# Per-head keys in a latent-attention trunk: one 128-row VectorE multiplication, with key rows and rope key copied into one tile by DMA

## The chip, the core and the metric

The kernel runs on one core of one Trainium2 chip. The core has five engines, each with its own row of instructions that it takes in order: TensorE (PE: matmuls, and PEld for the weight loads that overlap them), VectorE (DVE), ScalarE (ACT), GpSimd (POOL) and SyncE (SP, which here only issues DMAs). Data lies in HBM, in SBUF (128 partitions, written "rows" below) and in PSUM, where matmuls write. The metric is the device time of one execution in microseconds (us); the median of several is compared. A profile is one further execution, recorded by the hardware profiler.

## What is computed

Two layers over 528 tokens (16 meta tokens and 512 others), 1024 channels. Each has a pooling branch and an attention branch with 8 heads; each head's key has 64 channels of its own and 32 rotary channels that all heads share. Both are normalized together, per head and token:

```python
k_nope, v = kv[..., :QK_NOPE_DIM], kv[..., QK_NOPE_DIM:]
k_pe = jnp.broadcast_to(k_rope_raw[:, :, None, :], (B, L, N_HEADS, QK_ROPE_DIM))
k = jnp.concatenate([k_nope, k_pe], axis=-1)
q = rmsnorm(q, g_qn)
k = rmsnorm(k, g_kn)
q = jnp.concatenate([q[..., :QK_NOPE_DIM], apply_rope(q[..., QK_NOPE_DIM:], pos)], axis=-1)
k = jnp.concatenate([k[..., :QK_NOPE_DIM], apply_rope(k[..., QK_NOPE_DIM:], pos)], axis=-1)
o = causal_block_attention(q, k, v)
```

All of it is float32. The attention's output is gated, projected, merged with the pooling branch and added to the residual stream.

## The kernel before

**Precision.** Every product is made of three matmuls (`mm3`, lines 188, 191 and 192): both factors are split into a high part (a ScalarE copy to fp32r, `whi`, `kh`, `th`) and a remainder (a VectorE subtraction, `wlo`, `kl`, `tl`), and high x high, high x low and low x high are summed in PSUM. So every weight tile that is loaded (`raw`, line 115, three buffers) costs ScalarE one copy (line 183) and VectorE one subtraction (line 184) before TensorE can use it, and its buffer is free for the next load after the subtraction.

**What sets the order.** The program is written as one stream of weight tiles (`stream`, `plan`), into which the attention's work is put at points given by counted matmul time (`step`, `fill`, `after`). The instruction order on each engine is then decided by a scheduler that plays the program through with its own estimates of durations; so a changed instruction can shift others around it. On the chip, each engine takes its row in order and waits on semaphores.

**Keys.** All tiles hold channels in rows and tokens in columns (528). A pair p of heads has a tile `kn[p]`: rows 0 to 63 hold the 64 own channels of the even head 2p, rows 64 to 127 those of the odd head 2p+1 (`ev_k`). `kp` holds the 32 rotary channels four times over, in rows 0 to 127 (`rope`, lines 534 and 535, GpSimd). The norm's factor per head and token is a row in HBM (`kdr`); `spread_k` (line 838) broadcasts it over 128 rows into `bc`, two heads ahead, on SyncE's queue.

**prep(h)** (line 842) makes one head's key: a tile `kf` whose 64 own rows are kn[p] x bc, a VectorE multiplication (line 849), and whose other 64 rows are kp x bc, a GpSimd multiplication (line 850). An even head has its own rows in 0 to 63 and the rotary ones in 64 to 127, an odd head the other way round; the matching rows of the query tile `qhl` are zero where a rotary copy is not wanted. `kf` is then split into `kh` (ScalarE, line 297) and `kl` (VectorE, line 298), and the query's rows are put together, the rotary ones by two DMAs between SBUF tiles (line 860).

**head(h)** (line 863) makes the scores S from `kh`, `kl` and `qhl`, masks them and finds the row minimum on VectorE (line 879), takes the exponential on ScalarE (line 886), and divides by the row sums on GpSimd (lines 924 and 926). `pv` transposes the probabilities on TensorE (line 946), splits them, and multiplies by the values (951, 952). Between these stand the weight stream's matmuls. prep(h+1) comes about half way through head h. In layer 1 the stream that runs beside the attention is made of sums and differences of gate weights (`fast`, lines 601 to 646), which give VectorE more to do per matmul.

Of the kernel before, what the change touches and what calls it, by code (L numbers as in the profile page):

```python
# [72 lines left out]
def trunk(ctx, tc, xT, pos, win, wkr, wqb, wkb, wvb, wgr, wpu, wmu, wout, gains, const, yT):  # L73
    nc = tc.nc
    pe, act, dve, gp, sp = nc.tensor, nc.scalar, nc.vector, nc.gpsimd, nc.sync
# [11 lines left out]
    def nm(s):  # L87
        uid[0] += 1
        return f"{s}_{uid[0]}"

    def slot(tag, dt=F32, bufs=1, w=W):
        return sl.tile([P, w], dt, tag=tag, name=nm(tag), bufs=bufs)

    def tmp(w=W):
        return tp.tile([P, w], F32, tag="tmp", name=nm("tmp"), bufs=3)
# [200 lines left out]
    def split(hi, lo, src, a, b):  # L296
        act.activation(hi[:, a:b], src, AF.Copy)  # L297
        dve.tensor_sub(lo[:, a:b], src, hi[:, a:b].bitcast(F32))  # L298
# [5 lines left out]
    def newton(y, a, t):  # L304
        dve.tensor_single_scalar(y.bitcast(I32), a.bitcast(I32), 1, op=ALU.logical_shift_right)
        dve.tensor_scalar(y.bitcast(I32), y.bitcast(I32), -1.0, float(0x5F3759DF), op0=ALU.mult, op1=ALU.add)
        dve.tensor_scalar(a, a, -0.5, None, op0=ALU.mult)
        for _ in range(3):
            dve.tensor_mul(t, y, y)
            dve.tensor_mul(t, t, a)  # L310
            dve.scalar_tensor_tensor(out=y, in0=t, scalar=1.5, in1=y, op0=ALU.add, op1=ALU.mult)
# [47 lines left out]
    class Layer:  # L359
# [158 lines left out]
        def k_factors(self):  # L518
            flat = lambda d: d.rearrange("h (s c) -> (h s) c", c=T // 16)
            na, ny, nt = (sm.tile([P, T // 16], F32, tag=t, name=nm(t)) for t in ("ka", "ky", "kt"))  # L520
            sp.dma_start(na, flat(ksr[self.l]))
            dve.tensor_scalar(na, na, 1.0 / QK, EPS, op0=ALU.mult, op1=ALU.add)
            newton(ny, na, nt)
            sp.dma_start(flat(kdr[self.l]), ny)
            self.bcs = {}
            for h in range(2):
                self.spread_k(h)

        def rope(self, out, src, a, b):
            n = b - a  # L530
            t = tmp()
            dve.stream_shuffle(t[:, :n], src, SWAP)
            dve.tensor_mul(t[:, :n], t[:, :n], tsin[:, a:b])
            gp.tensor_mul(src, src, tcos[:, a:b])
            gp.tensor_add(out, src, t[:, :n])
# [302 lines left out]
        def spread_k(self, h):  # L838
            self.bcs[h] = bc = slot("bc", bufs=3)
            sp.dma_start(bc, kdr[self.l][h:h + 1, :].partition_broadcast(P))  # L840

        def prep(self, h):
            p, odd = h // 2, h % 2
            n0, r0 = (64, 0) if odd else (0, 64)
            kf = tmp()
            bc = self.bcs.pop(h)
            if h + 2 < H:
                self.spread_k(h + 2)
            dve.tensor_mul(kf[n0:n0 + 64, :], self.kn[p][n0:n0 + 64, :], bc[n0:n0 + 64, :])
            gp.tensor_mul(kf[r0:r0 + 64, :], self.kp[r0:r0 + 64, :], bc[r0:r0 + 64, :])  # L850
            kh, kl = slot("kh", F32R, bufs=2), slot("kl", F32R, bufs=2)
            split(kh, kl, kf[:, :T], 0, T)
            qh, ql = qhl[odd]
            x0 = self.x0
            src = self.qn[p][n0:n0 + 64, x0:T]
            act.activation(qh[n0:n0 + 64, x0:T], src, AF.Copy)
            dve.tensor_sub(ql[n0:n0 + 64, x0:T], src, qh[n0:n0 + 64, x0:T].bitcast(F32))
            g0 = 32 * (h % 4)
            for d, f in zip((qh, ql), self.qr[h // 4]):
                sp.dma_start(d[r0:r0 + 32, x0:T].bitcast(F32), f[g0:g0 + 32, x0:T].bitcast(F32))  # L860
            return kh, kl, qh, ql
# [551 lines left out]
```

## Time and profile before

| | us |
|---|---|
| median of 3 runs (lowest, highest) | 786.03 (784.74, 787.63) |
| the profiled execution: its time | 788.06 |
| the profiled execution: span, first to last instruction | 786.2 |
| attention of layer 0 in it (first and last key multiplication) | 154 to 285 |
| attention of layer 1 in it | 531 to 677 |
| granted TensorE clock, mean | 1.000 |

In the profile's lines, `L184 DVE TENSOR_TENSOR wlo<-raw,whi 128x512` is the VectorE instruction of line 184 that writes a tile `wlo` from `raw` and `whi`. Groups give the count (x16), busy time, mean duration, and idle time of the engine before them with what ended it. A row of a timeline gives start and duration in us. A row of waits gives who waited for whom: us in total, times, longest. A matmul's end is modelled, so starts are safer to read than ends.

### The profile page before, as it was taken

The numbers are of one execution on the slowest core, as the hardware profiler recorded it, in microseconds if no ns is written. First come the engines' busy times: TensorE is split into PE (matmuls) and PEld (weight loads), VectorE is DVE, ScalarE is ACT, GpSimd is POOL, SyncE is SP. The second block draws the span as 40 slices with busy tenths as digits, with TensorE's granted clock in tenths as the row PEclk, the third lists the DMA queues.
The fourth block names the chain that finished last, engine by engine and source line by source line (L and its number), as shares of the span: only waits on it lengthen the run. The fifth ranks groups of instructions, "written<-read, shape, count | busy, mean of one in ns | idle before, by whom it ended". The sixth has DMA issues, their size and how long they took to land.

```text
span 786.2 us, 15369 instructions
## 1 busy us (share of the span) xinstructions
PE 774.8 (99%) x5469; PEld 711.1 (90%) x5469; DVE 587.0 (75%) x1316; ACT 446.7 (57%) x1022; POOL 230.2 (29%) x319
## 2 busy tenths in 40 slices
PE   9999999999999999999999999999999999999998
PEld 8999899999999999999997898887788899788887
DVE  5848788547778977689764477775997899974984
ACT  8545655645556665545664356455667676654462
POOL 1024514203434342211320245131026235240213
PEclk9999999999999999999999999999999999999999
DMA  6242367765645465565653423435456566562655
GB/s 243 82 97 87 103 163 165 180 154 136 144 120 138 120 135 150 135 187 155 172 151 92 102 81 95 125 88 181 121 132 162 160 168 164 150 212 88 213 148 136
DMA packets 64909, 110.76 MB, mean 141 GB/s; under 512 B 10544, under 2 KB 16560, under 8 KB 64832
## 3 DMA queue, kind: packets, MB, share of 16 engines
q1 hardware_dynamic: 54928, 90.02, 38.4%
q0 software_dynamic: 8896, 17.92, 12.6%
q10 hardware_dynamic: 1008, 1.84, 0.6%
q8 instruction: 43, 0.70, 0.4%
q14 instruction: 34, 0.28, 0.1%
HBM read 100.18 MB, written 22.62 MB: 156 GB/s over the span
## 4 chain that ended last, share of the span: by engine, by line
PE 84%; DVE 6%; DMA 4%; issue 2%; ACT 2%; POOL 0%; SPq 0%; DVEq 0%; ACTq 0%
PE mm L188 24%; PE mm L192 23%; PE mm L191 23%; DVE wlo L184 2%; PE S L188 2%; PE S L191 2%; PE S L192 2%; PE mm L946 2%; DMA raw<-wsumgp 1%; DMA raw<-win 1%; PE o L952 1%; PE o L951 1%; PE S L500 1%; ACT whi L183 1%; DMA raw<-wqb 1%
## 5 line engine op out<-in xcount | busy, mean ns | idle before, releaser
L188 PE MATMUL mm<-hh,whi 128*128 128x264 f32 (+2 forms) x992 | 306.0, 311 | 1.6 <-DVE tmp L637 0.6
L192 PE MATMUL mm<-hh,wlo 128*128 128x264 f32 (+2 forms) x992 | 304.1, 309 | 1.1 <-DVE wlo L184 1.0
L191 PE MATMUL mm<-hl,whi 128*128 128x264 f32 (+2 forms) x992 | 304.5, 308 | 0.0
L184 DVE TENSOR_TENSOR wlo<-raw,whi 128x512 fp32r<-128x512 f32 (+2 forms) x261 | 191.9, 739 | 98.1 <-ACT whi L183 94.3
L183 ACT ACTIVATE whi<-raw 128x512 fp32r<-128x512 f32 (+2 forms) x261 | 156.5, 603 | 165.9 <-PE mm L191 91.0
L188 PEld LDWEIGHTS mm<-hh,whi 128*128 128x128 f32 x992 | 186.2, 188 | 12.9 <-issue 1.2
L192 PEld LDWEIGHTS mm<-hh,wlo 128*128 128x128 f32 x992 | 185.8, 188 | 10.6 <-DVE wlo L184 2.3
L191 PEld LDWEIGHTS mm<-hl,whi 128*128 128x128 f32 x992 | 186.8, 188 | 9.1
L188 PE MATMUL mm<-cq,whi 128*128 128x264 f32 (+2 forms) x140 | 44.2, 316 | 1.3 <-ACT racc L960 0.7
L192 PE MATMUL mm<-cq,wlo 128*128 128x264 f32 (+2 forms) x140 | 43.5, 313 | 0.6 <-DVE wlo L184 0.6
L191 PE MATMUL mm<-cq,whi 128*128 128x264 f32 (+2 forms) x140 | 43.5, 312 | 0.0
L879 DVE CUSTOM_DVE_ANT_0 S<-S,maskw,nqs 128x288 f32<-128x288 f32 (+4 forms) x80 | 38.4, 497 | 2.5 <-PE S L192 2.2
L702 POOL TENSOR_TENSOR racc<-racc,tmp 128x264 f32<-128x264 f32 (+1 forms) x15 | 14.3, 951 | 87.2 <-ACT tmp L701 87.1
L188 PE MATMUL mm<-u,whi 128*128 128x264 f32 (+1 forms) x108 | 35.3, 327 | 0.1
L192 PE MATMUL mm<-u,wlo 128*128 128x264 f32 (+1 forms) x108 | 34.8, 322 | 0.0
L298 DVE TENSOR_TENSOR tl<-mm,th 128x512 fp32r<-128x512 f32 (+1 forms) x64 | 29.2, 481 | 7.4 <-ACT th L297 6.3
L850 POOL TENSOR_TENSOR tmp<-kp,bc 64x528 f32<-64x528 f32 x16 | 25.6, 1602 | 30.5 <-issue 15.4
L353 POOL DMA_DIRECT2D wsum<-wout x8 | 6.9, 859 | 89.0 <-PE mm L192 73.0
L924 POOL TENSOR_TENSOR pm<-pa,rs 128x16 f32<-128x16 f32 x32 | 11.0, 345 | 72.6 <-DVE rs L919 66.7
L926 POOL TENSOR_TENSOR cq<-cq,rs 128x384 f32<-128x384 f32 (+1 forms) x32 | 32.2, 1005 | 0.0
L886 ACT ACTIVATE cq<-S,bia 128x400 f32<-128x400 f32 (+2 forms) x48 | 24.6, 515 | 12.2 <-DVE bia L914 7.2
L297 ACT ACTIVATE th<-mm 128x512 fp32r<-128x512 f32 (+1 forms) x64 | 25.9, 432 | 8.4 <-PE mm L946 7.3
(333 smaller groups left out, 1722.0 us busy)
## 6 DMA issues: line engine op xcount, KB each, us to landing
raw<-win SPq DMA_DIRECT2D x139, 256.0 KB, 3.0
raw<-wout SPq DMA_DIRECT2D x22, 256.0 KB, 3.5
bc<-kdr SPq DMA_DIRECT2D x16, 264.0 KB, 4.2
wsum<-wout SPq DMA_DIRECT2D x16, 256.0 KB, 3.5
raw<-wpu SPq DMA_DIRECT2D x16, 256.0 KB, 3.1
wsumgp<-win SPq DMA_DIRECT2D x16, 256.0 KB, 3.3
raw<-wmu SPq DMA_DIRECT2D x16, 256.0 KB, 2.7
raw<-wsumgp SPq DMA_DIRECT2D x16, 256.0 KB, 3.8
```

The lines of the kernel that those rows point to most:

```text
L183: act.activation(hi[:, :n], raw[:, :n], AF.Copy)
L184: dve.tensor_sub(lo[:, :n], raw[:, :n], hi[:, :n].bitcast(F32))
L188: first = pe.matmul(out, wh, xh, start=start, stop=False, skip_group_check=more)
L191: pe.matmul(out, wh, xl, start=False, stop=False, skip_group_check=more)
L192: newest[0] = pe.matmul(out, wl, xh, start=False, stop=stop, skip_group_check=more)
L297: act.activation(hi[:, a:b], src, AF.Copy)
L298: dve.tensor_sub(lo[:, a:b], src, hi[:, a:b].bitcast(F32))
L850: gp.tensor_mul(kf[r0:r0 + 64, :], self.kp[r0:r0 + 64, :], bc[r0:r0 + 64, :])
L879: dve.tensor_tensor_reduce(out=sv, in0=sv, in1=mask, scale=nqs[:, i, h:h + 1], scalar=3e38, op0=ALU.add, op1=ALU.min, accum_out=bia[:, c:c ...
L886: act.activation(pv, sv, AF.Exp, scale=-1.0, bias=bia[:, i:i + 1], accum_out=rs[:, c:c + 1])
L926: gp.tensor_mul(pt[i][:, NM:], pt[i][:, NM:], rs[:, i:i + 1].to_broadcast([P, n - NM]))
L946: pe.transpose(tr[:, P * (i - j):P * (i - j + 1)], pt[i][:, NM + P * j:NM + P * (j + 1)], ident)
```

## The change

```diff
@@ k_factors, after the loop over spread_k(0), spread_k(1)
+            self.lend(0)
 
@@ beside spread_k
+        def lend(self, p):
+            sp.dma_start(self.kp[0:64, :], self.kn[p][0:64, :])
+
         def prep(self, h):
             p, odd = h // 2, h % 2
             n0, r0 = (64, 0) if odd else (0, 64)
@@ in prep
             bc = self.bcs.pop(h)
             if h + 2 < H:
                 self.spread_k(h + 2)
-            dve.tensor_mul(kf[n0:n0 + 64, :], self.kn[p][n0:n0 + 64, :], bc[n0:n0 + 64, :])
-            gp.tensor_mul(kf[r0:r0 + 64, :], self.kp[r0:r0 + 64, :], bc[r0:r0 + 64, :])
+            dve.tensor_mul(kf, self.kn[p] if odd else self.kp, bc)
+            if not odd:
+                sp.dma_start(self.kn[p][0:64, :], self.kp[64:128, :])
+            elif p < 3:
+                self.lend(p + 1)
```

A pair's first copy (`lend`) puts the even head's own rows into rows 0 to 63 of `kp`, whose rows 64 to 127 keep the rotary key: `kp` is then the whole key of the even head. The second copy puts the rotary key from `kp` into rows 0 to 63 of `kn[p]`, whose rows 64 to 127 hold the odd head's own channels. Each head is then one VectorE multiplication over all 128 rows. Per layer there are 8 copies of 64 x 528 float32. The first copy of pair p+1 waits for the multiplication of head 2p, which reads `kp`; the second copy of a pair waits for the first one, which reads the rows it overwrites.

The scheduler's order changes with it. On SyncE, in layer 1's attention, the rows around the broadcast (`bc`) for head 6 stood like this before (`raw` are weight tiles, `kdr` the norm factors; numbers tell buffers apart and may differ by one between the two programs):

```order
L115 DMA raw_8565<-wsumgp_124 128x512
L840 DMA bc_8764<-kdr_122 128x528
L115 DMA raw_8585<-wsumgp_124 128x512
L115 DMA raw_8639<-win 128x512
L115 DMA raw_8661<-win 128x512
```

In the changed program (its line numbers are higher by 1 to 7) the same place reads:

```order
L115 DMA raw_8566<-wsumgp_124 128x512
L841 DMA bc_8765<-kdr_122 128x528
L844 DMA kp_6474<-kn_1215_6722 64x528
L115 DMA raw_8586<-wsumgp_124 128x512
L855 DMA kn_1215_6722<-kp_6474 64x528
L115 DMA raw_8640<-win 128x512
L115 DMA raw_8662<-win 128x512
```

Both copies of the last pair stand among the weight loads, right behind the broadcast that is set free by head 4's multiplication, with one weight load between them; two weight loads stand behind the second copy. In the other pairs the second copy follows the first directly (the first two pairs of each layer), or with one to three DMAs between.

On TensorE, the first score products of head 6 of layer 1 (S from `kh_9005` before, `kh_9006` in the changed program) stood at the end of a gate tile's 24 matmuls (`mm_9104`, `mm_9105`), which before began and ended so:

```order
L188 MATMUL mm_9104<-hh_6_132,whi_9058 128x512
L191 MATMUL mm_9104<-hl_7_133,whi_9058 128x512
L192 MATMUL mm_9104<-hh_6_132,wlo_9059 128x512
...
L192 MATMUL mm_9104<-hh_20_146,wlo_9101 128x512
L952 MATMUL o_8865<-tl_9025,vt 128x128
L946 MATMUL mm_9122<-cst,pa_8814 128x128
L188 MATMUL S_9082<-kh_9005,qhl_105 128x272
L188 MATMUL S_9091<-kh_9005,qhl_105 128x400
```

In the changed program the tile begins:

```order
L188 MATMUL mm_9105<-hh_6_132,whi_9059 128x512
L191 MATMUL mm_9105<-hl_7_133,whi_9059 128x512
L188 MATMUL S_9083<-kh_9006,qhl_105 128x272
L188 MATMUL S_9092<-kh_9006,qhl_105 128x400
L188 MATMUL S_9173<-kh_9006,qhl_105 128x288
L192 MATMUL mm_9105<-hh_6_132,wlo_9060 128x512
L188 MATMUL mm_9105<-hh_8_134,whi_9059 128x512
```

The three products with `kh` moved ahead of 22 of the tile's matmuls; those with `kl` follow at the tile's end, as before. Similar moves stand at heads 3 and 5 of layer 1 and, smaller ones, at heads 2 and 3 of layer 0. The rows of GpSimd keep their order without the sixteen multiplications.

## The prediction

> **What bounds the kernel now.** First the page: busy times, then the chain that ended last.
>
> ```profile
> span 786.2 us, 15369 instructions
> ...
> PE 774.8 (99%) x5469; PEld 711.1 (90%) x5469; DVE 587.0 (75%) x1316; ACT 446.7 (57%) x1022; POOL 230.2 (29%) x319
> ...
> PE 84%; DVE 6%; DMA 4%; issue 2%; ACT 2%; POOL 0%; SPq 0%; DVEq 0%; ACTq 0%
> ```
>
> TensorE is busy for 99% of the span and carries 84% of the chain. The change takes no matmul away, so it can only win where TensorE stands still. The busy times by stretch say where that is.
>
> ```profile
> core 0: us, PE busy (x) PEld busy (x) DVE busy (x) ACT busy (x) POOL busy (x), PEclk, DMA share, GB/s
> 200.00:220.00 20.00, 20.00 (x165) 19.78 (x165) 15.80 (x42) 12.23 (x31) 7.68 (x11) 1.00 0.61 145
> 640.00:660.00 20.00, 19.79 (x141) 18.30 (x140) 19.82 (x44) 14.79 (x38) 8.56 (x11) 1.00 0.57 131
> ```
>
> In layer 0's attention (200 to 220 us stands for it) TensorE has no idle time: eight of the sixteen heads can win nothing. In layer 1's attention (640 to 660) VectorE is nearly full, 19.82 of 20 us, and TensorE has holes. Who ends them stands in the view of waits, for TensorE alone (total, times, longest):
>
> ```profile
> PE mm L192 <- DVE wlo L184: 1.6, 3, 0.8
> ...
> PE mm L188 <- ACT racc L960: 0.7, 1, 0.7
> ...
> PE mm L188 <- DVE tmp L637: 0.6, 1, 0.6
> PE o L951 <- DVE tmp L967: 0.6, 1, 0.6
> ```
>
> These 1.6 + 0.7 + 0.6 + 0.6 = 3.5 us are what the change has to work on.
>
> **The change, part by part.** *The multiplications.* Sixteen GpSimd multiplications go (L850); sixteen of VectorE (L849) become 128 rows high.
>
> ```profile
> L850 POOL TENSOR_TENSOR tmp<-kp,bc 64x528 f32<-64x528 f32 x16 | 25.6, 1602 | 30.5 <-issue 15.4 <-DVE xb L717 6.6 <-DVE rs L918 6.5
> L849 DVE TENSOR_TENSOR tmp<-kn,bc 64x528 f32<-64x528 f32 x16 | 16.1, 1008 | 0.3
> L849 DVE TENSOR_TENSOR tmp<-kn,bc x16: 668/705/1756, 156.0 to 676.0; 64x528 f32<-64x528 f32 x16
> L298 DVE TENSOR_TENSOR kl<-tmp,kh 128x528 fp32r<-128x528 f32 x16 | 11.2, 703 | 4.9 <-ACT kh L297 4.8
> ```
>
> A VectorE operation over 128 x 528 with two inputs takes 0.70 us (kl), as much as the 64-row multiplication at its median (0.705): twice the rows cost nothing. The price of one lies between 0.67 and 1.76 (the ends of L849); I take 0.70. That GpSimd's 25.6 us go is worth nothing on GpSimd, which holds 0% of the chain. It is worth something by what ran beside it:
>
> ```profile
> 531.49 1.82 DVE L184 TENSOR_TENSOR wlo<-raw,whi 128x512 fp32r<-128x512 f32 x1
> 531.09 1.66 POOL L850 TENSOR_TENSOR tmp<-kp,bc 64x528 f32<-64x528 f32 x1
> 533.36 0.51 PE L192 MATMUL mm<-cq,wlo 128*128 128x512 f32 x1 [0.64 <-DVE wlo L184]
> 609.70 1.59 DVE L849 TENSOR_TENSOR tmp<-kn,bc 64x528 f32<-64x528 f32 x1
> 609.68 1.04 POOL L926 TENSOR_TENSOR cq<-cq,rs 128x512 f32<-128x512 f32 x1
> 611.31 1.70 DVE L184 TENSOR_TENSOR wlo<-raw,whi 128x512 fp32r<-128x512 f32 x1
> 610.68 1.78 POOL L850 TENSOR_TENSOR tmp<-kp,bc 64x528 f32<-64x528 f32 x1
> 613.66 0.50 PE o L951
> 668.50 1.52 DVE L184 TENSOR_TENSOR wlo<-raw,whi 128x512 fp32r<-128x512 f32 x1
> 670.28 1.80 DVE L184 TENSOR_TENSOR wlo<-raw,whi 128x512 fp32r<-128x512 f32 x1
> 669.55 1.99 POOL L850 TENSOR_TENSOR tmp<-kp,bc 64x528 f32<-64x528 f32 x1
> 670.07 0.50 PE L192 MATMUL mm<-hh,wlo 128*128 128x512 f32 x1 [0.79 <-DVE wlo L184]
> 672.11 5.20 DMA raw<-wsumgp
> 681.82 0.38 PE mm L188
> ```
>
> The weight remainders (wlo) take 1.82, 1.70, 1.52 and 1.80 us where L850 runs beside them, against 0.70 for kl, which is the same subtraction and longer. That is 1.12 + 1.00 + 0.82 + 1.10 = 4.0 us too much, each right ahead of a hole of TensorE: 0.64 at 533; 0.6 at 613.66 (through L967, behind the wlo of 611.31); 0.79 at 670. The last one frees its buffer 1.1 us late, so that the load of 672.11 (in the chain, 5.20 us) starts late, and behind it stands the 0.7 at 681.82. L637's hole and the rest of wlo's come between these, in the same loop of load, split and matmul, which runs 1.0 us late from 611 on. So all of the 3.5 us hang on VectorE's lateness by L850; I credit them whole. Since a matmul's end is modelled, a hole costs somewhat more than its idle time; I leave that as cover for new waits.
>
> Not all of L849's own excess goes: 16.1 - 16 x 0.705 = 4.8 us, part of it made by L926, as at 609.70; I count half as L850's. [...]
>
> *The copies.* Sixteen DMAs of 64 rows, 64 x 528 x 4 B = 132 KB each, on SyncE's queue. No row has their size between SBUF tiles; the nearest are the query rows of 66 KB (two lines) and the broadcasts of 264 KB (the last line):
>
> ```profile
> L860 SPq DMA_DIRECT2D qhl<-q x32: 507/535/597, 137.2 to 659.1; - x32
> ...
> DMA to landing us min/median/max: 1.9/2.8/5.0
> DMA to landing us min/median/max: 3.4/4.2/6.0
> ```
>
> So 0.54 us of SyncE each, landing after 1.9 to 6.0; I take 2.8, as for the smaller ones between tiles. [...] The data is in time: the copy for a head goes out when the head two before it has been multiplied. What is dangerous is the wait: the second copy of a pair overwrites what the first one reads, so SyncE stands until the first has landed, with the weight loads queued behind it. Mostly those loads are early: the one behind the pair after head 0 of layer 1 was issued at 553.19 and split from 561.00 on, 7.8 us later. The tight place is the pair after head 4, from 629 on:
>
> ```profile
> 553.19 0.33 SPq L115 DMA_DIRECT2D raw<-win  x1
> ...
> 561.00 0.63 ACT L183 ACTIVATE whi<-raw 128x512 fp32r<-128x512 f32 x1 [0.63 <-ACT hh L297]
> ...
> 629.29 0.33 SPq L840 DMA_DIRECT2D bc<-kdr  x1
> 634.07 1.00 SPq L115 DMA_DIRECT2D raw<-win  x2
> 639.78 0.62 ACT L183 ACTIVATE whi<-raw 128x512 fp32r<-128x512 f32 x1
> ```
>
> The first copy goes at about 629.6, right behind the broadcast; with 2.8 us the second goes at 632.4, and the two loads of 634.07 lose nothing. From a landing of 4.4 us on (634.07 - 629.6) they go late; at 6.0 by 1.6 + 0.54 = 2.1 us, against 0.5 of slack ahead of the split at 639.78 (a load of 5.20, as above, lands at 639.3). Cost 0 to 1.6 us; I take 0.
>
> *What moves.* The order of every engine's instructions shifts for the earlier key, most at head 6 of layer 1: its first score products stood behind the eight matmul triples of a gate tile, and now stand behind its second matmul.
>
> ```profile
> 668.89 0.39 PE L191 MATMUL mm<-hl,whi 128*128 128x512 f32 x1
> 667.86 0.71 DVE L849 TENSOR_TENSOR tmp<-kn,bc 64x528 f32<-64x528 f32 x1
> 667.47 0.63 ACT L183 ACTIVATE whi<-raw 128x512 fp32r<-128x512 f32 x1
> 671.57 0.65 ACT L297 ACTIVATE kh<-tmp 128x528 fp32r<-128x528 f32 x1 [1.35 <-POOL tmp L850]
> ```
>
> TensorE reaches them at 669.1 (behind the matmul of 668.89). The key's high part stood ready at 672.2; with L850 gone the multiplication ends at 668.57, the whi ahead of it on ScalarE at 668.10, and kh at 669.2. So this costs 0.1 us where it works, up to 3.1 where the key comes as late as now. I take 0.
>
> **Sum.** The profiled execution took 788.06 us, 786.2 of span and 1.9 around it. Its span becomes 786.2 - 3.5 = 782.7, its time 784.6. It is 2.0 above the median of the runs (786.03), so for a median I forecast 786.03 - 3.5 = **782.5 us**.
>
> **The rivals.** *Swallowed:* only the hole at 533 goes, since it has nothing but wlo ahead of it; in 610 to 682 the loop's other links (loads of 5.2 us, ScalarE's row) end last instead. For it: that load stands in the chain with 5.20 us and no engine shortens it. 786.0 - 0.6 = 785.4.
>
> *All of VectorE's time counts:* in 640 to 660 it is full to 99%. Then the 4.0 us of wlo and half of L849's 4.8 come off: 786.0 - 6.4 = 779.6. Against it: the holes shown hold 3.5.
>
> *The order is made for a key that doesn't come early (slower):* the wide multiplication is held by L926 and by VectorE's own row, kh comes at 672.2 as now, and TensorE, which takes its row in order, stands at head 6 for 3.1 us. No hole closes. 786.0 + 3.1 = 789.1. It decides once kh is over 0.1 us later than 669.1. For it: the 1.59 at 609.70. Against: at 667.86 L849 took 0.71.
>
> **How the numbers follow.** Forecast 0.50 (gains of 2 to 5 us), swallowed 0.21, all of VectorE 0.19, slower 0.10. A measurement of this kernel can tell about 0.5%, 3.9 us, from no change: the bound is 782.1. Below it lie two fifths of the forecast (0.20) and nearly all of the third case (0.18): faster 0.38. Slower by over 0.5% (789.96) is half of the last: 0.05. The rest, 0.57, is within. The range of 779.0 to 788.0 holds the forecast, the swallowed case, the copies' 1.6 us and most of the third; out of it are the last and the third's lower end, together under 0.2.
>
> **What would show it.** Right: no wlo of layer 1 over 1.2 us outside L926 and the rotary steps; VectorE's multiplications at 0.70 with a few at 1.6; TensorE's waits for wlo, L967 and L637 gone; layer 0's attention as long as before. Wrong: a wait of TensorE for kh or kl; weight loads waiting behind a copy; copies that land after more than 4.4 us. A gain in layer 0 would overturn the reading that TensorE is full there.

## The result, and the profile after

| | before | after |
|---|---|---|
| median of 21 runs each (lowest, highest), us | 786.03 (784.16, 787.63) | 784.24 (782.94, 786.42) |
| the profiled execution: time, us | 788.06 | 783.18 |
| the profiled execution: span, us | 786.2 | 781.4 |

The medians differ by 1.8 us. The ratio over all runs is 0.9981, with a 95% interval of 0.9973 to 0.9989, which is 1.5 us (0.9 to 2.1): a real gain, and about half of the 3.5 us that were forecast. The predicted time, 782.5, lies 1.7 below the measured one; the range held it. The two profiled executions stand further apart than the medians, 4.9 us: that of before was 2.0 above its median, that of after 1.1 below. Whoever compares only these two profiles finds the forecast more than confirmed.

The page of the changed kernel, busy times and chain:

```profile
span 781.4 us, 15357 instructions
...
PE 774.5 (99%) x5469; PEld 711.6 (91%) x5469; DVE 579.4 (74%) x1316; ACT 445.5 (57%) x1022; POOL 206.7 (26%) x303
...
PE 90%; DMA 5%; DVE 3%; ACT 1%; issue 1%; ACTq 0%; DVEq 0%
```

TensorE's busy time is as before (774.8), GpSimd is 23.5 us shorter, VectorE 7.6, and the span has lost almost only TensorE's idle time. The waits of TensorE in 520 to 695 us, layer 1's attention with its edges (total, times, longest):

```profile
PE o L958 <- DVE tmp L974: 0.7, 1, 0.7
PE mm L192 <- DVE wlo L184: 0.2, 1, 0.2
```

The four waits of the forecast's sum (wlo 1.6, racc 0.7, L637 0.6, L967 0.6) have shrunk to 0.2. A new one of 0.7 has come: `o` waits for the addition in line 974 (967 before). The changed lines, first the groups (busy, mean ns; idle time ahead), then the copies, from two views of their lines and SyncE's waits:

```profile
L853 DVE TENSOR_TENSOR tmp<-kp,bc 128x528 f32<-128x528 f32 x8 | 6.7, 839 | 0.0
L853 DVE TENSOR_TENSOR tmp<-kn,bc 128x528 f32<-128x528 f32 x8 | 6.7, 837 | 0.0
L297 ACT ACTIVATE kh<-tmp 128x528 fp32r<-128x528 f32 x16 | 10.2, 637 | 0.4 <-DVE tmp L853 0.4
```

```profile
L844 SPq DMA_DIRECT2D kp<-kn x8: 502/507/558, 82.5 to 626.7; - x8
DMA to landing us min/median/max: 2.6/4.4/5.7
L855 SPq DMA_DIRECT2D kn<-kp x8: 482/500/504, 85.2 to 631.1; - x8
SPq L855 <- DMA kp<-kn: 24.8, 8, 4.5
```

A multiplication over 128 rows has a median of 0.70 us by the view of its line, as forecast; the sixteen take 13.4 us together. No wlo of over 1.2 us in layer 1's attention is left but beside GpSimd's divisions (L933) and the rotary steps. ScalarE waits 0.4 us for the key in all (L297); in the first profile of before it was 6.4 us for L850 and 3.3 for L849:

```profile
L297 ACT ACTIVATE kh<-tmp 128x528 fp32r<-128x528 f32 x16 | 10.3, 643 | 9.9 <-POOL tmp L850 6.4 <-DVE tmp L849 3.3
```

A pair's first copy lands after 4.4 us at the median, not 2.8 as forecast, and SyncE stands 24.8 us behind the eight; the second copies land after 2.7.

Two theories were put against each other. **One execution:** the 3.5 us of holes were partly those of one execution, and a usual one has fewer. **Given back:** the holes are there each time and close, but the copies take half of it back.

### The profile page after: what moved, and what is told of

The parts are those of the page before. It is cut to its first block, busy times and chain, and to the rows that moved or that the text cites. A ratio compares the mean times of both kernels' runs of the same rounds, so it can differ in the third digit from the quotient of the medians.

```text
span 781.4 us, 15357 instructions
## 1 busy us (share of the span) xinstructions
PE 774.5 (99%) x5469; PEld 711.6 (91%) x5469; DVE 579.4 (74%) x1316; ACT 445.5 (57%) x1022; POOL 206.7 (26%) x303
## 4 chain that ended last, share of the span: by engine, by line
PE 90%; DMA 5%; DVE 3%; ACT 1%; issue 1%; ACTq 0%; DVEq 0%
PE mm L188 26%; PE mm L192 25%; PE mm L191 25%; PE S L188 2%; PE S L191 2%; PE S L192 2%; PE mm L953 2%; DMA raw<-win 2%; PE o L959 1%; PE o L958 1%; DVE wlo L184 1%; PE S L500 1%; DMA raw<-wqb 1%; DMA xb<-xT 1%; PE mm L402 1%
## 5 line engine op out<-in xcount | busy, mean ns | idle before, releaser
L886 DVE CUSTOM_DVE_ANT_0 S<-S,maskw,nqs 128x272 f32<-128x272 f32 (+4 forms) x80 | 38.4, 497 | 5.0 <-PE S L192 4.6
L931 POOL TENSOR_TENSOR pm<-pa,rs 128x16 f32<-128x16 f32 x32 | 11.4, 355 | 92.7 <-DVE rs L926 71.6
L933 POOL TENSOR_TENSOR cq<-cq,rs 128x384 f32<-128x384 f32 (+1 forms) x32 | 32.9, 1027 | 0.0
L297 ACT ACTIVATE th<-mm 128x512 fp32r<-128x512 f32 (+1 forms) x64 | 26.2, 432 | 9.5 <-PE mm L953 9.0
L191 PE MATMUL mm<-kn,whi 128*128 128x264 f32 (+1 forms) x96 | 30.6, 320 | 0.0
```

Source lines behind the costliest of these rows:

```text
L191: pe.matmul(out, wh, xl, start=False, stop=False, skip_group_check=more)
L886: dve.tensor_tensor_reduce(out=sv, in0=sv, in1=mask, scale=nqs[:, i, h:h + 1], scalar=3e38, op0=ALU.add, op1=ALU.min, accum_out=bia[:, c:c ...
L933: gp.tensor_mul(pt[i][:, NM:], pt[i][:, NM:], rs[:, i:i + 1].to_broadcast([P, n - NM]))
```

## The experiments

The twelve ran in three groups of four, each group on one chip, with the kernel before timed beside them. A number that the experiments share is worked out from the traces: for every pair of neighbouring matmuls the time from start to start, less the usual time for the first one's width (the median, 0.231 us for 512 columns; for 128 columns, whose median is 0.108, a shorter 0.06), where that is over 0.1 us. Its sum over 520 to 695 us is called TensorE's **lost time in layer 1**. With 0.108 for 128 columns every entry is 0.1 to 0.6 lower, and their order stays.

| kernel | lost time in layer 1, us, one profile each |
|---|---|
| before | 7.8, 5.2, 6.3, 5.6 |
| changed in layer 0 alone (layer 1 in the order of before) | 5.6 |
| changed | 3.0, 3.3, 3.5 |
| changed in layer 1 alone | 3.6 |
| changed, without copies | 3.5, 4.1 |
| changed, GpSimd beside it | 5.1 |
| changed, head 7's multiplication moved back | 4.6 |

### The kernel before, three more profiles

No edit. The expectations of the second, third and fourth profile:

> The kernel before, unchanged, for a second profile of it. Theory ONE EXECUTION (the forecast's 3.5 us of holes were those of one execution that was 2.0 us above the median; a usual execution has fewer): TensorE's idle time (span less busy, 11.4 us in the first profile) comes out 1 us or more lower, and its waits for wlo, racc L960, tmp L637 and tmp L967 sum to under 2.6 us. Theory GIVEN BACK (the holes are there in every execution and close, but the 16 copies cost about 1.7 us elsewhere): the four waits sum to 3.0 to 4.0 us again.

> The kernel before, a third profile. ONE EXECUTION: holes at 532 and 613 again, those at 669 and 681 not both.

> The kernel before, a fourth profile. ONE EXECUTION: holes at 532 and 613 again, those at 669 and 681 not both.

TensorE's waits in 520 to 695 us, in the second, third and fourth profile:

```profile
PE mm L192 <- DVE wlo L184: 0.9, 2, 0.7
PE o L951 <- DVE tmp L967: 0.6, 1, 0.6
PE mm L188 <- DVE sv L627: 0.3, 1, 0.3
```

```profile
PE mm L192 <- DVE wlo L184: 1.3, 3, 0.7
PE o L951 <- DVE tmp L967: 0.6, 1, 0.6
...
```

```profile
PE mm L192 <- DVE wlo L184: 0.9, 2, 0.7
PE o L951 <- DVE tmp L967: 0.6, 1, 0.6
...
PE mm L188 <- DVE tmp L637: 0.2, 1, 0.2
```

TensorE's idle time in the second profile is 783.6 - 775.6 = 8.0 us, not 11.4. The four waits sum to 1.5, 1.9 and 1.7 us, not 3.5; the wait for racc is in none of them. In every profile the hole behind the wlo at 532 and the one behind L967 at 613 stand unmoved; the other half came and went. Why shows in the second profile, VectorE and GpSimd around the same three places:

```profile
531.39 1.67 POOL L850 TENSOR_TENSOR tmp<-kp,bc 64x528 f32<-64x528 f32 x1
531.78 1.82 DVE L184 TENSOR_TENSOR wlo<-raw,whi 128x512 fp32r<-128x512 f32 x1
611.00 1.79 POOL L850 TENSOR_TENSOR tmp<-kp,bc 64x528 f32<-64x528 f32 x1
611.63 1.71 DVE L184 TENSOR_TENSOR wlo<-raw,whi 128x512 fp32r<-128x512 f32 x1
...
666.64 1.28 POOL L926 TENSOR_TENSOR cq<-cq,rs 128x384 f32<-128x384 f32 x1
667.16 1.31 DVE L184 TENSOR_TENSOR wlo<-raw,whi 128x512 fp32r<-128x512 f32 x1
```

At 531 and 611 the wlo meets L850 as in the first profile, to 0.01 us. At 667 it meets L926 and takes 1.31; the pair of 1.52 and 1.80 at 668.50 and 670.28, which the forecast counted, is not there. Counted over 520 to 695, L850 lies beside five wlo's of over 1.5 us in the first profile, and beside two, two and three in the others. ONE EXECUTION holds, with one reserve: the third profile has a lesser hole at 669 (0.64 from start to start, behind L926), and in all three a wait for sv stands at 682 to 684 in place of that for racc (0.6 from start to start, where racc's was 0.9).

### The changed kernel again

Its second profile, and its second timing with a third profile:

> The changed kernel, unchanged, for a second profile of it (the first was 1.1 us below its median). ONE EXECUTION: TensorE's idle time is about 1 us above the 6.9 us of the first profile, with holes at other places. GIVEN BACK: 6.9 us within 0.5, with the same holes as in the first profile, the largest (0.7 us, o of L958 for tmp of L974) among them.

> The changed kernel, unchanged, timed again on the chip of the next three kernels. The first comparison gave 0.9981 (0.9973 to 0.9989). ONE EXECUTION: 0.998 again, within 0.001. If it comes out at 0.9995, as the kernel without copies did on another chip, the gain depends on the chip.

The second profile's idle time is 783.0 - 773.2 = 9.8 us (6.9 in the first), more than ONE EXECUTION had said, and the additional holes lie mostly in the first 130 us (waits for hh 1.6 and for tmp of L702 1.0), ahead of both attentions. In layer 1 the same holes stood again, the wait of 0.7 for L974 in all three profiles; there GIVEN BACK's expectation was the better one. The second timing gave 783.89 against 785.26, ratio 0.9989 (0.9980 to 0.9998): 1.4 us by the medians, 0.9 by the ratio. By the record this group ran on the chip of the first group, so the 0.9995 of the kernel without copies, told next, is not that of another chip, as the expectation takes it to be. The kernel before had medians of 784.5 to 786.0 in the four comparisons; small gains are to be read with that in mind.

### Without the copies

```diff
-            self.lend(0)
...
-            if not odd:
-                sp.dma_start(self.kn[p][0:64, :], self.kp[64:128, :])
-            elif p < 3:
-                self.lend(p + 1)
```

> The changed kernel without its 16 copies between SBUF tiles: even heads use kp as it stands (rotary rows in place of own rows), odd heads kn as it stands (the even head's rows in place of rotary rows), so keys and output differ; all other instructions stay. GIVEN BACK: the copies' 1.7 us come off the changed kernel's 784.2, so 782.5, ratio to before 0.9955. ONE EXECUTION: the copies cost nothing, 784.2 within 0.6, ratio 0.9977 (0.997 to 0.9985).

> The changed kernel without its 16 copies (even heads use kp as it stands, odd heads kn as it stands, so keys and output differ), again, now beside the changed kernel on one chip; the order on TensorE, VectorE and ScalarE is exactly the changed kernel's. GIVEN BACK: 1 us or more faster than the changed kernel. Copies free: within 0.6 us of it.

The first group gave 783.89 against 784.47, ratio 0.9995 (0.9984 to 1.0006), above both expectations and not to be told from no gain; the second group, beside the changed kernel, 783.83 against that one's 783.89, ratio to before 0.9985 (0.9976 to 0.9994). The copies cost 0.1 us there, with an uncertainty of about 1: 1.7 us for them is not what was measured, and the changed kernel without them shows no smaller lost time (3.5 and 4.1). GIVEN BACK falls. The wait for L974 is as long without them (0.7), so it is not theirs.

### GpSimd put back beside the changed kernel

```diff
             dve.tensor_mul(kf, self.kn[p] if odd else self.kp, bc)
+            src = self.kn[p] if odd else self.kp
+            gp.tensor_mul(bc[r0:r0 + 64, :], src[r0:r0 + 64, :], bc[r0:r0 + 64, :])
```

> The changed kernel with a GpSimd multiplication of the old shape (64 rows x 528) behind each VectorE one, into bc, whose data nobody reads any more; the output stays, and the order on TensorE, VectorE and ScalarE is exactly that of the changed kernel. So GpSimd's 25 us come back beside VectorE, and off the key's path. Theory CONTENTION (GpSimd beside wlo is what the change took away): the gain of about 1.8 us is lost again, ratio to the kernel before 0.9995 to 1.001, with wlo's of 1.5 us and over in layer 1's attention. Rival ORDER AND KEY (the gain comes of the earlier key and the other order): the ratio is that of the changed kernel within 0.0008.

785.32 us, ratio 1.0012 (1.0000 to 1.0024), in the group in which the changed kernel gave 0.9989 (0.9980 to 0.9998). The instructions of TensorE, VectorE and ScalarE stand in one order in both, and in layer 1 the key comes as early (within 0.1 us) for the first six heads, and 1.75 us later, with VectorE's row, for the last two; GpSimd's work alone costs 1.4 us by the medians, 1.8 by the two ratios. The whole gain is gone. CONTENTION holds, ORDER AND KEY falls. In 520 to 695 us the same VectorE instructions are busy for 152.09 us (the third busy time), where the changed kernel's two profiles shown further down have 148.94 and 148.38:

```profile
520.00:695.00 175.00, 172.53 (x1031) 149.56 (x1030) 152.09 (x341) 115.62 (x283) 62.00 (x84) 1.00 0.59 163
```

The new instruction also holds the broadcast's buffer longer. That is not the path of the loss: in the same stretch SyncE waits 3.0 us for it, and 4.9 for VectorE's multiplication in the changed kernel; ScalarE's wait for weight loads is 9.7 us, between the 7.0 and 11.2 of two profiles of the changed kernel. The new GpSimd groups, and TensorE's waits in 520 to 695 us (line numbers 2 higher from there on):

```profile
L855 POOL TENSOR_TENSOR bc<-kn,bc 64x528 f32<-64x528 f32 x8 | 13.1, 1635 | 29.3 <-DVE tmp L853 16.9 <-DVE rs L928 12.4
L855 POOL TENSOR_TENSOR bc<-kp,bc 64x528 f32<-64x528 f32 x8 | 12.2, 1519 | 28.7 <-issue 25.5 <-DVE tmp L853 2.7 <-DVE rs L927 0.2
```

```profile
PE mm L188 <- DVE tmp L638: 1.0, 1, 1.0
PE o L960 <- DVE tmp L976: 0.7, 1, 0.7
PE o L961 <- DVE tl L298: 0.5, 1, 0.5
```

The holes are at other places than in the kernel before, since GpSimd's instruction now comes behind VectorE's. The 0.7 is the changed kernel's own, and the 1.0, the longest, has no L855 in the 11 us ahead of it; a wait of 0.5 to 0.6 at its place also stands in some kernels without this instruction (told below). The third begins here, again in VectorE's and GpSimd's rows:

```profile
646.19 0.85 POOL L935 TENSOR_TENSOR pa<-pa,rs 128x128 f32<-128x128 f32 x1
646.71 2.59 DVE L184 TENSOR_TENSOR wlo<-raw,whi 128x512 fp32r<-128x512 f32 x1
647.19 0.60 POOL L935 TENSOR_TENSOR pa<-pa,rs 128x256 f32<-128x256 f32 x1
```

The wlo stands beside a row of GpSimd's divisions and takes 2.59 us, tl goes late (at 649.23), and TensorE waits 0.5 for it. That GpSimd's added work pushed these divisions against the wlo fits the rows, but wasn't tried by itself. Only one wlo of over 1.5 us stands beside an L855 (1.55 at 627.36). So that GpSimd's work costs the time is shown; which hole carries how much of it is not.

### The change in one layer

```diff
-            dve.tensor_mul(kf, self.kn[p] if odd else self.kp, bc)
+            if self.l == 1:
+                dve.tensor_mul(kf, self.kn[p] if odd else self.kp, bc)
...
+            else:
+                dve.tensor_mul(kf[n0:n0 + 64, :], self.kn[p][n0:n0 + 64, :], bc[n0:n0 + 64, :])
+                gp.tensor_mul(kf[r0:r0 + 64, :], self.kp[r0:r0 + 64, :], bc[r0:r0 + 64, :])
```

The copies go with it; the other kernel has `self.l == 0`.

> The change in layer 1 alone; layer 0 makes its keys as before, with GpSimd and without copies. By the prediction's reading TensorE is full in layer 0's attention and all of the gain lies in layer 1: the ratio is that of the changed kernel within 0.0008. If layer 0 has a share, it is 0.999 or above.

> The change in layer 0 alone; layer 1 keeps GpSimd's multiplication and, from 400 us on, exactly the order of the kernel before. TensorE is full in layer 0's attention: ratio 1.000 within 0.0008, and layer 1 shows the holes of the kernel before, so its profile is one more look at those: the fixed ones behind wlo at 532 and L967 at 613, 0.8 to 0.9 us each from one matmul's start to the next; those at 625, 669 and 681 (0.8 to 0.95 in the first profile, gone or smaller in the second) in some profiles only, by ONE EXECUTION.

Layer 1 alone: 784.16 against 785.26, ratio 0.9993 (0.9981 to 1.0005); layer 0 alone: 785.05 against 784.68, ratio 0.9996 (0.9986 to 1.0007). By the times neither can be told from the other; the profiles can. Layer 1 alone has the lost time of the changed kernel (3.6), layer 0 alone that of before (5.6, with the hole at 532 and one of 0.93 at 613, where TensorE waited for kh in place of L967). In 150 to 520 us every profile of every kernel here lost 2.1 to 2.9 us, the changed ones no less than those of before. So no gain in layer 0 is shown.

### Both multiplications on VectorE

```diff
-            gp.tensor_mul(kf[r0:r0 + 64, :], self.kp[r0:r0 + 64, :], bc[r0:r0 + 64, :])
+            dve.tensor_mul(kf[r0:r0 + 64, :], self.kp[r0:r0 + 64, :], bc[r0:r0 + 64, :])
```

> The kernel before with the GpSimd multiplication of 64 rows made by VectorE: no copies, no GpSimd multiplication, 16 x 0.70 us more on VectorE, 5.6 of it in layer 1's attention where VectorE is nearly full. ONE EXECUTION: GpSimd's removal is worth 1.8 us in the median, and up to 1.5 of it goes to VectorE's longer row: 784.2 to 786.0. GIVEN BACK: removal is worth 3.5, so 782.5 to 784.0.

791.79 us, ratio 1.0102 (1.0084 to 1.0120): slower by 7.3, outside both expectations. So it decides nothing between the theories. The scheduler made an order of its own, with the first score products of head 2 right behind those of head 1; TensorE lost 5.3 us there (580 to 620; 1.4 to 2.0 in the profiles of before), 1.3 of them by a lower clock, which is told at the end. Here a shorter row on GpSimd was no gain by itself; that VectorE's does not grow for it is what the copies are for.

### The new wait for L974

In the changed kernel VectorE's row has head 7's multiplication, which nobody is waiting for, ahead of the addition that empties `o`; here with TensorE's row that waits for it:

```profile
673.45 0.70 DVE L853 TENSOR_TENSOR tmp<-kn,bc 128x528 f32<-128x528 f32 x1
674.07 0.64 DVE L886 CUSTOM_DVE_ANT_0 S<-S,maskw,nqs 128x400 f32<-128x400 f32 x1
674.62 0.47 DVE L886 CUSTOM_DVE_ANT_0 S<-S,maskw,nqs 128x240 f32<-128x240 f32 x1
675.01 0.68 DVE L974 TENSOR_TENSOR tmp<-o,tmp 64x512 f32<-64x512 f32 x1
675.83 0.47 PE L958 MATMUL o<-th,vt 128*128 128x512 f32 x1 [0.67 <-DVE tmp L974]
```

```diff
-            dve.tensor_mul(kf, self.kn[p] if odd else self.kp, bc)
+            mul = dve.tensor_mul(kf, self.kn[p] if odd else self.kp, bc)
+            if self.l == 1 and h == 7:
+                behind(mul, self.added)
```

`self.added` is the last such addition.

> The changed kernel with the multiplication of head 7 of layer 1 put behind the addition L974 that empties o for head 5's products (it stood ahead of it, where every profile of the changed order has a hole of 0.87 us, o of L958 waiting for tmp of L974). Theory ORDER (this hole is made by the moved order, and takes back half of what the fixed holes gave): the hole falls to about 0.25, since two of the mask steps still stand ahead of L974, and the time by 0.3 to 0.7 us, to a ratio 0.0004 to 0.0009 below the changed kernel's 0.9981 to 0.9989, unless the shifted rows behind it make another. Rival: the hole stays, since L974's input comes late.

The hole of 0.87 fell to 0.26 as ORDER said, so it is the row's order that makes it. The time did not follow: 783.80 against 784.68, ratio 0.9987 (0.9977 to 0.9998), the changed kernel's. In this kernel's profile other holes stand in layer 1, ahead of the moved instruction (0.85 at 624 and 0.49 at 621; a hole at 623 also stands in some profiles of the changed order and not in others). A gain of 0.6 us can't be told from none here, and no version that beats the changed one was found.

## What the prediction had right, and the step that failed

**What bounds the kernel: right.** TensorE bounds it, layer 0 gives nothing that could be measured, and layer 1's holes are where the gain was. In 520 to 695 us (busy times by stretch; the first number behind the length is TensorE's) the four profiles of before, then the first and third of the changed kernel, read:

```profile
520.00:695.00 175.00, 171.13 (x1021) 147.56 (x1020) 150.40 (x340) 114.57 (x280) 58.69 (x80) 1.00 0.57 154
520.00:695.00 175.00, 173.07 (x1032) 149.64 (x1031) 151.23 (x343) 116.02 (x282) 62.30 (x82) 1.00 0.58 159
520.00:695.00 175.00, 172.25 (x1027) 148.82 (x1026) 151.15 (x341) 115.31 (x281) 61.06 (x81) 1.00 0.58 156
520.00:695.00 175.00, 172.60 (x1030) 149.38 (x1029) 151.94 (x343) 116.38 (x282) 62.19 (x83) 1.00 0.59 159
```

```profile
520.00:695.00 175.00, 173.98 (x1040) 151.12 (x1039) 148.94 (x345) 116.09 (x286) 51.56 (x76) 1.00 0.59 165
520.00:695.00 175.00, 173.52 (x1038) 150.85 (x1037) 148.38 (x345) 116.17 (x286) 51.44 (x76) 1.00 0.59 165
```

The first profile of before, the only one that the forecast had, is the one with the most idle time: 3.9 us against 1.9 to 2.8.

**The mechanism: right, for two of the holes.** GpSimd's multiplications beside VectorE's work cost time here: put back in one and the same order, they cost 1.4 us. By the rows L850 made the holes at 532 and 613 (the wlo's beside it took 1.82 and 1.70 us, the median wlo of 525 to 690 us 0.69), which stand in all four profiles of before and in none of the changed kernel.

**The mis-sized term: "So all of the 3.5 us hang on VectorE's lateness by L850; I credit them whole."** In three further profiles these waits are 1.5 to 1.9 us, and the measured gain is 1.8 by the medians and 1.5 by the ratio (1.4 and 0.9 in the second comparison).

One part of the term was misread, and the first profile shows it. The wlo of 668.50, ahead of the hole of 0.79 at 670, was put down to the L850 of 669.55. But this wlo began 1.05 us before that L850, and 0.53 behind the start of this division:

```profile
667.97 1.50 POOL L926 TENSOR_TENSOR cq<-cq,rs 128x512 f32<-128x512 f32 x1
```

The division ended at 669.47 and the wlo at 670.02, 0.55 behind it; the wlo's of 531.49, 611.31 and 670.28 ended 0.54 to 0.56 behind the end of the L850 that had begun before them. So the 0.79 stood behind a division, which the change leaves in place. Nor does L637's 0.6 need L850. In the second profile without copies, where GpSimd multiplies no keys, TensorE waits for the same statement:

```profile
PE mm L188 <- DVE tmp L637: 0.6, 1, 0.6
```

With layer 1 alone changed it waits 0.5 for that statement, with head 7's multiplication moved 0.6. What hung on L850 each time is 0.64 + 0.6 = 1.2 us of idle time, 1.6 of lost time; the step that failed is to credit the rest as well.

The rest was also this execution's: racc's 0.7, behind the load of 672.11, is in none of the other profiles. The working had put the profile's 2.0 us above the median into the base (786.03 for 788.06) but not into the term: the 2.0 us that made that execution long were, by the profiles, mostly the holes that the term counted. (The execution of the third profile was 2.1 above its group's median with waits of 1.9, so a long execution need not have these holes.) Between the lost times, the first profiles differ by 7.8 - 3.0 = 4.8 us, the medians of all (5.6 of five with layer 1 as before, 3.4 of four with it changed) by 2.2. Of these, 1.6 are the two holes, and the new wait for L974 takes 0.9 back; so some 1.5 come of lesser holes that stand in some profiles only, and which of them hang on L850 isn't shown. Why VectorE and GpSimd met as they did at 668 to 674 in that execution was not settled.

**"A hole costs somewhat more than its idle time; I leave that as cover for new waits": right in kind.** The wait at 532 is 0.64 and its lost time 0.8. It was needed: the moved order made the new wait of 0.7 for L974.

**What moves, taken as 0: too low, at another place.** At head 6 TensorE waited 0 to 0.4 us for kh in the changed kernel's profiles (0.1 was forecast); the cost came 9 us later, from the same move, as the wait for L974. The text had looked only at those who wait for the key, not at who stands behind the multiplication in VectorE's row.

**The copies, taken as 0: right in cost, as far as an uncertainty of 1 us tells, and wrong in size.** The tight pair after head 4, SyncE's row:

```profile
626.32 0.32 SPq L841 DMA_DIRECT2D bc<-kdr  x1
626.69 0.51 SPq L844 DMA_DIRECT2D kp<-kn  x1
627.46 0.37 SPq L115 DMA_DIRECT2D raw<-wsumgp  x1
631.11 0.50 SPq L855 DMA_DIRECT2D kn<-kp  x1
631.71 1.06 SPq L115 DMA_DIRECT2D raw<-win  x2
```

This copy landed after 4.4 us, exactly the bound from which it was to hurt. But it went out 2.9 us earlier than was reckoned (626.7, not 629.6), since the broadcast ahead of it goes at 626.3 now instead of 629.3, and the two loads went at 631.71, not at 634.07 or later. Two of the prediction's signs of being wrong did show, without a cost that could be measured: copies that landed after more than 4.4 us (5.7 at most), and TensorE's wait for kh in one of three profiles.

**L849's excess, half credited: right.** 16.1 us became 13.4, so the excess over 16 x 0.70 fell from 4.9 to 2.2. The longest of the new ones began 0.50 us behind the start of a GpSimd division and ended 0.56 behind its end:

```profile
624.25 1.48 POOL L933 TENSOR_TENSOR cq<-cq,rs 128x512 f32<-128x512 f32 x1
624.75 1.54 DVE L853 TENSOR_TENSOR tmp<-kp,bc 128x528 f32<-128x528 f32 x1
```

The other three of over 0.8 us (1.37 at 224.70, 1.14 at 608.13, 0.94 at 206.46) each began behind the start of an L933, too, and ended 0.55 to 0.56 behind its end, as in the first profile of before L849's 1.59 of 609.70 ended 0.57 behind the L926 of 609.68. The four make up the 2.2 that is left; the half was an estimate.

**The rivals.** *Swallowed* (785.4) and the forecast (782.5) lie on the two sides of the measured 784.24: neither the loads nor the other links took the place of the closed holes at 532 and 613, but of the rest the 0.79 at 670 was not L850's to close, and the others come and go. *All of VectorE's time counts* is out: VectorE lost 7.6 us, the kernel 1.8. *A key not early* is out: ScalarE's wait for it fell to 0.4 us.

## What to carry to other kernels

A sum of holes out of one profile holds that execution's chances too: where the profiled execution lies above the median, take a second profile before crediting holes, and count only those that stand in both. Before a long VectorE instruction is put down to one of GpSimd's, look for the one that began before it, and whether VectorE's ended just behind that one's end (in the cases above 0.54 to 0.57 us behind it). Where VectorE's work stands ahead of a TensorE that has no slack, look at the GpSimd work beside it: here a wlo, with two inputs of 128 x 512, took 1.70 to 1.82 us behind an L850 that had begun before it, against 0.69 at the median, and moving such work away paid 1.5 to 1.8 us of 786 although GpSimd was idle 70% of the time, and with it put into VectorE's row as further instructions (and in another order) the kernel was 7.3 us slower. When an order moves, look also at who stands behind the moved instruction in its own engine's row.

## What the runs showed of the hardware that was not expected

In the kernel with both multiplications on VectorE, more was lost around TensorE's standstill than the standstill itself. The stretches around it (length, busy times of TensorE, its weight loads, VectorE, ScalarE and GpSimd, granted clock, DMA share, GB/s):

```profile
593.50:595.20 1.70, 0.28 (x4) 0.13 (x3) 1.70 (x8) 1.65 (x5) 0.07 (x1) 1.00 0.99 282
595.20:596.20 1.00, 0.96 (x5) 0.76 (x6) 0.97 (x2) 0.41 (x2) 1.00 (x2) 1.00 0.83 287
596.20:597.70 1.50, 0.96 (x7) 0.58 (x5) 1.45 (x6) 0.35 (x1) 1.50 (x5) 0.83 0.07 23
597.70:601.50 3.80, 3.80 (x13) 3.05 (x12) 1.84 (x6) 1.63 (x8) 3.42 (x9) 0.62 0.01 2
```

Over 4.2 us TensorE was busy for 0.28 + 0.96 + 0.96 = 2.2; then the mean granted clock was 0.62 over 3.8 us (0.53 in 597 to 600), and 1.00 again from 601.5 to 603. The 512-column matmuls of 598.3 to 600.0 start 0.42 to 0.43 us apart, against the usual 0.231, and the stretch lost 1.3 us by it while TensorE shows as busy. TensorE's longest idle time in 590.5 to 600 was 1.42 us (up to 595.20), and the clock fell behind a stretch in which TensorE was busy half of the time. That this stretch is the cause fits the one profile, but was not tried.
